# A decoder trunk on one core: x loaded ahead of the weights, and the first gate tile in two groups of k tiles

## The chip, the core and the metric

The kernel runs on one core of a Trainium2 chip. The metric is the device time of one execution in microseconds (us). A core has five engines that run their own queues of instructions: PE (TensorE, matrix products and transposes), DVE (VectorE), ACT (ScalarE), POOL (GpSimd) and SP (SyncE, which here issues nearly all DMAs). PEld in the profile is PE's loading of the operand that stays in the array.

## The reference: what is computed

Two layers of a trunk over 256 tokens with 1024 channels, in float32. Each layer is a half-step feed-forward block, a mixer of three groups of attention heads, and a second half-step feed-forward block. The change lies in the first feed-forward block of the first layer:

```
def rms_norm(x, g):
    y = xf * lax.rsqrt(jnp.mean(xf * xf, axis=-1, keepdims=True) + RMS_EPS)
    return (y * g.astype(jnp.float32)).astype(x.dtype)

def swiglu(x, w_gate, w_up, w_down):
    return (jax.nn.silu(x @ w_gate) * (x @ w_up)) @ w_down

h = h + 0.5 * swiglu(rms_norm(h, ffn1_norm[l]), ffn1_w_gate[l], ffn1_w_up[l], ffn1_w_down[l])
```

The gate and up matrices are 1024 x 2816, the down matrix 2816 x 1024.

## The kernel before

**Products in two parts.** A float32 operand is split in two fp32r tiles: a high part, which is a cast, and a low part, which is the float32 value minus the high part. A product is the sum of three: high by high, high by low, low by high. For weights, `W.high()` makes `wh` on ACT (line 117) and `W.low()` makes `wl` on DVE (line 121). For the activations, class `Norm` holds `xhl`, a tile of 8 k tiles by (high, low) by 256 tokens; `Norm.high` (line 318, ACT) multiplies the transposed x by the norm's gain and writes the high part, `Norm.low` (line 321, DVE) writes the low part. The division by the root of the mean square is applied later, behind the projection (`norm.sums`, `norm.broadcast`).

**A projection tile.** A tile of 128 hidden columns of gate or up takes, in `proj` (line 396), eight products of `wh` with high and low of x at once (512 columns, called wide here) into the two halves of one PSUM bank, and then eight products of `wl` with the high part (256 columns, called narrow) into the first half. `summed` (line 431) adds the halves.

**Loads.** All weights go through raw buffers that SP fills (line 91) in a fixed order, five in flight. x goes to `trunk` (token by channel) and is turned on PE with four 128 x 128 transposes per two k tiles (`Norm.turn`, line 324, transposes at line 329).

**The opening**, written out by hand. The constants with the identity matrix come on ACT's queue. SP issues: first quarter of x (256 of 1024 channels, 1 KB runs), lower half of the first gate tile (k tiles 0 to 3, 256 KB), second quarter of x, upper half of the gate tile, third and fourth quarters of x, the first up tile, the second gate tile, the second up tile. PE starts with 7 warm-up products of ones by ones, whose result nobody reads (line 1096), and then follows lines 1121 to 1138:

- `turn_x(0)`, the gains turned (`turn_gains`), 7 more warm-up products, `turn_x(1)`;
- for each quarter of x: its two products of `wh` by high (256 columns), two quarters ahead the next `turn_x`, then the products of `wl` by high, then of `wh` by low. The third and the fourth quarter are turned between the products of the first and the second.

ACT casts a half of the gate tile (line 1118) and then writes the high parts of a quarter; POOL subtracts to get `wl` of the gate tile (line 1119); DVE writes the low parts. Behind the gate tile (`g0`) `ffn` starts with the first up tile (`u0 = proj()`), then `g1`, `u1` and so on. ACT goes on with the casts of the next weights, then with the squares of x for the norm (line 344).

Of the kernel before, what the change touches and what calls it, by code (L numbers as in the profile page):

```python
# [18 lines left out]
P = 128  # L19
S = 256  # L20
D = 1024
KT = D // P
# [15 lines left out]
WARM = 7  # L38
# [103 lines left out]
def kernel(ctx: ExitStack, tc: tile.TileContext, x, ffn1_norm, ffn1_w_gate, ffn1_w_up, ffn1_w_down,  # L142
# [15 lines left out]
    V, A, G, T = nc.vector, nc.scalar, nc.gpsimd, nc.tensor  # L158

    def bank(tag):  # L160
        return psum.tile([P, 512], F32, name="ps_" + tag, tag=tag)
# [13 lines left out]
    def turn_gains(i):  # L175
        ps = bank("gu")
        T.transpose(ps[:, :16], rows[i], ident[:16, :16])
        V.tensor_copy(gT[:, 16 * i:16 * i + 16], ps[:, :16])

    ones = cp.tile([P, P], F32, name="ones")  # L180
# [2 lines left out]
    G.memset(minus_half, -0.5)  # L183
    nc.scalar.dma_start(cst[:, 0:P], const[:, 0:P])

    def load_x(mp):
        cols = slice(256 * mp, 256 * mp + 256)
        nc.sync.dma_start(trunk[:, :, cols], x[0].rearrange("(t p) d -> p t d", p=P)[:, :, cols])  # L188

    load_x(0)  # L190
    load_gains(0, ffn1_norm, nc.scalar)
    A.activation(tmp(P), ones, AF.Exp)
# [9 lines left out]
    W = Weights(tc, raw_pool, split_pool)  # L202
# [55 lines left out]
    W.by_hand = 2  # L258
    W.n_raw_done -= RAW_BUFS - 2
    W.issue()  # L260
    for mp in range(1, 4):
        if mp < 3:
            W.load(0, mp - 1)
        load_x(mp)
    W.load(1, 0)
    W.load(0, 2)
    W.load(1, 1)
# [25 lines left out]
    def mm(o, l, r, start, stop):  # L293
        T.matmul(o, l, r, start=start, stop=stop, skip_group_check=True)  # L294
# [789 lines left out]
    def before_mixer(l):  # L1084
        if l == 0:
            turn_gains(1)
            turn_gains(2)
            V.tensor_copy(identr, ident)
            V.memset(causal[:, P:2 * P], 0.0)
            for t in range(2):  # L1090
                V.tensor_scalar(causal[:, 2 * t * P:(2 * t + 1) * P], future, NEG, None, op0=ALU.mult)
        mixer_tables(l)

    warm = bank("gu")
    for i in range(WARM):
        mm(warm[:, :P], ones, ones, i == 0, i == WARM - 1)
    norm = Norm(0, 0)
    src, wh, wl = W.high_tiles()
    g0 = bank("gu").rearrange("p (a b) -> p a b", a=2)
    xT = []  # L1100

    def turn_x(mp):
        xT.append(norm.turn(mp))

    def gate(w, xs, ks):
        for k in ks:
            mm(g0[:, int(xs is norm.l)], w[:, k], xs[:, k], w is wh and xs is norm.h and k == 0,
               xs is norm.l and k == KT - 1)

    def first_norm(mp):  # L1110
        for i in range(2):
            norm.high(2 * mp + i, xT[mp][:, i])
        for i in range(2):
            norm.low(2 * mp + i, xT[mp][:, i])

    def split_gate(hf):
        ks = slice(4 * hf, 4 * hf + 4)
        A.copy(wh[:, ks], src[:, ks])
        G.tensor_tensor(wl[:, ks], src[:, ks], wh[:, ks].bitcast(F32), op=ALU.subtract)

    turn_x(0)
    turn_gains(0)
    for i in range(WARM):
        mm(warm[:, P:2 * P], ones, ones, False, i == WARM - 1)
    split_gate(0)
    first_norm(0)
    turn_x(1)
    split_gate(1)
    for mp in range(4):
        ks = range(2 * mp, 2 * mp + 2)  # L1130
        gate(wh, norm.h, ks)
        if mp < 2:
            turn_x(mp + 2)
        if mp > 0:
            gate(wl, norm.h, range(4) if mp == 1 else ks)
        gate(wh, norm.l, ks)
        if mp < 3:
            first_norm(mp + 1)
    W.low_done()
    W.take()  # L1140
    W.high()
# [8 lines left out]
    for l in range(DEPTH):  # L1150
        norm = ffn(norm, lambda: Norm(1, l), lambda: before_mixer(l), g0 if l == 0 else None)
        norm = mixer(l, norm, lambda: Norm(2, l))
        norm = ffn(norm, (lambda: Norm(0, l + 1)) if l + 1 < DEPTH else None)
# [35 lines left out]
```

## Time and profile before

| | |
|---|---|
| median of 3 runs | 1041.9 us (1041.54 to 1042.21) |
| the profiled execution's own time | 1041.75 us |
| its span, first to last instruction | 1039.8 us |
| HBM read | 179.67 MB, 174 GB/s over the span |
| ACT in the first 2.5% of the span | busy 6 tenths |
| DVE in the first 2.5% of the span | busy 4 tenths |

How to read the rows further down: in a timeline, the first number is the start in us from the start of the span, the second how long it took, then engine, line, operation, the tiles as out<-in, how many instructions the row merges, and in brackets how long the engine sat idle ahead of it and what ended that. A row that merges several instructions lasts from the first's start to the last's end. The ends of products are modelled and overlap the next one, so costs on PE are read from start to start. A row of DMA issues gives size and time from issue to landing. A row of a windows view gives the stretch, its length, the busy time and count of PE, PEld, DVE, ACT and POOL, the granted clock, the DMA engines' busy share and GB/s.

### The profile page before, as it was taken

The page shows a single profiled execution, that of the slowest core. Times are in us where ns is not written, and L with a number is a line of the kernel's source. Part 1 is how long each engine was busy: PE and PEld are TensorE (multiplying, and loading weights), DVE is VectorE, ACT ScalarE, POOL GpSimd, SP SyncE. Part 2 cuts the span into 40 slices and gives each one's busy share as a digit, 9 for nine tenths or more (in the row PEclk, how much of TensorE's full clock was granted, in tenths as well). Part 3 has the DMA queues.
Part 4 walks back from the last instruction along what each step waited for, and adds up shares of the span by engine and source line. Part 5 has one row for each costly group of instructions (what it writes and reads, how often), then busy time and mean ns, then how long its engine had stood idle before and what let it go on. Part 6 is the DMA issues. An engine that isn't in the chain of part 4 may idle for free.

```text
span 1039.8 us, 15145 instructions
## 1 busy us (share of the span) xinstructions
PE 1034.6 (100%) x5659; PEld 899.4 (86%) x5659; DVE 808.5 (78%) x1536; ACT 594.9 (57%) x1047; POOL 142.7 (14%) x173
## 2 busy tenths in 40 slices
PE   9999999999999999999999999999999999999998
PEld 8888888898888888888888888888988888888887
DVE  4997777789876887777788777777898768877775
ACT  6565555667754655555466555547667556555551
POOL 1003000167700000000000200002765000000000
PEclk9999999999999999999999999999999999999999
DMA  9675555555431374654646464555455214564631
GB/s 322 218 245 181 189 207 171 175 187 185 154 130 42 122 242 161 204 193 172 202 163 215 159 240 158 207 171 185 163 193 173 81 61 160 184 237 147 223 122 41
DMA packets 130905, 181.70 MB, mean 175 GB/s; under 512 B 7008, under 2 KB 104720, under 8 KB 130832
## 3 DMA queue, kind: packets, MB, share of 16 engines
q1 hardware_dynamic: 130656, 180.65, 51.0%
q8 instruction: 45, 0.74, 0.3%
q14 instruction: 28, 0.23, 0.1%
q10 hardware_dynamic: 176, 0.07, 0.0%
HBM read 179.67 MB, written 1.05 MB: 174 GB/s over the span
## 4 chain that ended last, share of the span: by engine, by line
PE 99%; DMA 1%; ACT 0%; SPq 0%; DVE 0%; issue 0%
PE ps_gu L294 66%; PE ps_acc L294 30%; PE ps_acc L329 1%; PE ps_gu L948 1%; PE ps_gu L1050 1%; DMA trunk<-in_x_dram 1%; PE ps_acc L649 0%; PE ps_acc L948 0%; PE ps_gu L981 0%; ACT wh L117 0%; SPq L91 0%; SPq L188 0%; PE ps_acc L355 0%; PE ps_acc L981 0%; DVE tmp L435 0%; DVE trunk L368 0%
## 5 line engine op out<-in xcount | busy, mean ns | idle before, releaser
L121 DVE TENSOR_TENSOR wl<-raw,wh 128x1024 fp32r<-128x1024 f32 (+2 forms) x343 | 416.6, 1220 | 29.2 <-ACT wh L117 29.0
L117 ACT CAST wh<-raw 128x1024 fp32r<-128x1024 f32 (+2 forms) x343 | 345.7, 1036 | 5.4 <-PE ps_gu L294 4.8
L294 PE MATMUL ps_gu<-xhl,wh 128*128 128x512 f32 (+1 forms) x1408 | 335.2, 389 | 0.2 <-DVE tmp L435 0.2
L294 PEld LDWEIGHTS ps_gu<-xhl,wh 128*128 128x128 f32 x1408 | 261.7, 188 | 53.2 <-DVE tmp L435 0.4
L294 PEld LDWEIGHTS ps_gu<-xhl,wl 128*128 128x128 f32 x1400 | 180.7, 191 | 7.2
L294 PE MATMUL ps_gu<-xhl,wl 128*128 128x256 f32 x1400 | 184.5, 283 | 0.0
L294 PE MATMUL ps_gu<-wh,xhl 128*128 128x512 f32 (+2 forms) x512 | 158.5, 379 | 0.0
L435 DVE TENSOR_TENSOR tmp<-ps_gu,tmp 128x256 f32<-128x256 f32 x175 | 72.5, 423 | 107.4 <-ACT tmp L434 107.2
L294 PE MATMUL ps_acc<-wh,hh 128*128 128x512 f32 (+1 forms) x352 | 137.7, 391 | 0.0
L294 PE MATMUL ps_acc<-wl,hh 128*128 128x512 f32 (+1 forms) x352 | 137.5, 391 | 0.0
L294 PE MATMUL ps_acc<-wh,hl 128*128 128x512 f32 (+1 forms) x352 | 136.5, 388 | 0.0
L434 ACT COPY tmp<-ps_gu 128x256 f32<-128x256 f32 x175 | 63.1, 371 | 93.9 <-PE ps_gu L294 93.8
L294 PEld LDWEIGHTS ps_gu<-wh,xhl 128*128 128x128 f32 x512 | 94.8, 188 | 14.5
L449 ACT CAST hh<-tmp 128x256 fp32r<-128x256 f32 x80 | 32.6, 407 | 119.9 <-DVE tmp L446 119.9
L294 PE MATMUL ps_gu<-wl,xhl 128*128 128x512 f32 (+2 forms) x256 | 95.7, 374 | 0.0
L305 POOL TENSOR_TENSOR y_n<-msq,minus_half 128x2 f32<-128x2 f32 x6 | 7.7, 1281 | 539.9 <-DVE msq L304 539.9
L441 ACT ACTIVATE tmp<-tmp 128x256 f32<-128x256 f32 x88 | 36.9, 419 | 77.8 <-DVE tmp L439 77.4
L294 PEld LDWEIGHTS ps_acc<-wh,hl 128*128 128x128 f32 x352 | 66.1, 188 | 14.0
L294 PEld LDWEIGHTS ps_acc<-wh,hh 128*128 128x128 f32 x352 | 66.4, 189 | 11.7
L294 PEld LDWEIGHTS ps_acc<-wl,hh 128*128 128x128 f32 x352 | 66.4, 189 | 11.4 <-DVE wl L121 0.7
L294 PEld LDWEIGHTS ps_gu<-wl,xhl 128*128 128x128 f32 x256 | 48.2, 188 | 6.6
L318 ACT ACTIVATE xhl<-ps_acc,gT 128x256 fp32r<-128x256 f32 x48 | 19.1, 475 | 37.2 <-PE ps_acc L329 37.1
(221 smaller groups left out, 1013.7 us busy)
## 6 DMA issues: line engine op xcount, KB each, us to landing
raw<-in_ffn_w_down_dram SPq DMA_DIRECT2D x44, 1024.0 KB, 4.9
raw<-in_ffn_w_gate_dram SPq DMA_DIRECT2D x43, 1024.0 KB, 6.7
raw<-in_ffn_w_up_dram SPq DMA_DIRECT2D x43, 1024.0 KB, 7.4
raw<-in_w_in_dram SPq DMA_DIRECT2D x24, 1024.0 KB, 5.0
raw<-in_w_out_dram SPq DMA_DIRECT2D x8, 1024.0 KB, 4.8
raw<-in_w_in_dram SPq DMA_DIRECT2D x4, 768.0 KB, 4.7
raw<-in_w_in_dram SPq DMA_DIRECT2D x4, 656.0 KB, 5.2
trunk<-in_x_dram SPq DMA_DIRECT2D x4, 256.0 KB, 4.7
```

The source lines that it names most:

```text
L117: self.nc.scalar.copy(hv, src)
L121: (engine or self.nc.vector).tensor_tensor(lv, self.srcs[self.n_low], hv.bitcast(F32), op=ALU.subtract)
L294: T.matmul(o, l, r, start=start, stop=stop, skip_group_check=True)
L305: G.tensor_tensor(y, dst, minus_half[:, :n], op=ALU.pow)
L318: A.activation(self.h[:, m], src, AF.Copy, scale=gT[:, self.col + m:self.col + m + 1])
L329: T.transpose(ps[:, i, t * P:(t + 1) * P], trunk[:, t, (2 * mp + i) * P:(2 * mp + i + 1) * P], ident)
L434: A.copy(o, ps[:, 1])
L435: V.tensor_tensor(o, ps[:, 0], o, op=ALU.add)
L441: A.activation(th, t_, AF.Tanh, scale=0.5)
L449: (V.tensor_copy if late else A.copy)(hh, t_)
L948: T.transpose(b[:, j * P:(j + 1) * P], pj[i][:, j * P:(j + 1) * P], ident)
L1050: T.transpose(b[:66, i * S + t * P:i * S + (t + 1) * P], src[t][:, 2 * hp_ + i, :], ident)
```

## The change

- x is loaded in two halves of 512 channels (2 KB runs), both issued ahead of every weight; then come both halves of the first gate tile, then the rest as before. SP issues two DMAs fewer.
- PE: 7 warm-up products as before; first quarter turned, gains turned, second quarter turned; 6 warm-up products; third and fourth quarter turned; 8 warm-up products. Only then the gate tile's products, in two groups of four k tiles: four wide products of `wh` with high and low, then four narrow ones of `wl` with high. That makes 8 products of 512 columns and 8 of 256 in place of 24 of 256, and 14 warm-up products in the place of 7 behind the first 7.
- ACT: the high parts of k tiles 0 to 3 come first, then the cast of the gate tile's lower half, then the high parts of k tiles 4 to 7.
- DVE: the low parts of k tiles 0 to 3, then the cast of the gate tile's upper half, which ACT did, then the low parts of k tiles 4 to 7.
- POOL: both subtractions as before.

```
-    def load_x(mp):
-        cols = slice(256 * mp, 256 * mp + 256)
+    def load_x(c):
+        cols = slice(512 * c, 512 * c + 512)
...
-    for mp in range(1, 4):
-        if mp < 3:
-            W.load(0, mp - 1)
-        load_x(mp)
+    load_x(1)
+    W.load(0, 0)
+    W.load(0, 1)
     W.load(1, 0)
...
+    def warm_up(n):
+        for i in range(n):
+            mm(warm[:, P:2 * P], ones, ones, False, i == n - 1)
...
-    def split_gate(hf):
+    def split_gate(hf, copy):
         ks = slice(4 * hf, 4 * hf + 4)
-        A.copy(wh[:, ks], src[:, ks])
+        copy(wh[:, ks], src[:, ks])
         G.tensor_tensor(wl[:, ks], src[:, ks], wh[:, ks].bitcast(F32), op=ALU.subtract)
...
-    turn_x(0)
-    turn_gains(0)
-    for i in range(WARM):
-        mm(warm[:, P:2 * P], ones, ones, False, i == WARM - 1)
-    split_gate(0)
-    first_norm(0)
-    turn_x(1)
-    split_gate(1)
-    for mp in range(4):
-        ks = range(2 * mp, 2 * mp + 2)
-        gate(wh, norm.h, ks)
-        if mp < 2:
-            turn_x(mp + 2)
-        if mp > 0:
-            gate(wl, norm.h, range(4) if mp == 1 else ks)
-        gate(wh, norm.l, ks)
-        if mp < 3:
-            first_norm(mp + 1)
+    for c in range(2):
+        xT.append(norm.turn(2 * c))
+        if c == 0:
+            turn_gains(0)
+        xT.append(norm.turn(2 * c + 1))
+        warm_up((6, 8)[c])
+        if c == 1:
+            split_gate(1, V.tensor_copy)
+        for mp in (2 * c, 2 * c + 1):
+            first_norm(mp)
+        if c == 0:
+            split_gate(0, A.copy)
+    for c in range(2):
+        for k in range(4 * c, 4 * c + 4):
+            mm(g0, wh[:, k], norm.x[:, k], k == 0, False)
+        for k in range(4 * c, 4 * c + 4):
+            mm(g0[:, 0], wl[:, k], norm.h[:, k], False, k == KT - 1)
```

More of the change, by code (lines that the diff above doesn't have):

```diff
@@ L1100 @@
     xT = []
[L1102 to L1108, printed above, removed]
+    def warm_up(n):
+        for i in range(n):
+            mm(warm[:, P:2 * P], ones, ones, False, i == n - 1)
     def first_norm(mp):
```

## The prediction

> **What bounds the kernel now.** I read the page's busy rows first, then its chain of work that ended last, then the list of waits of PE from 12 us to the end.
>
> ```profile
> span 1039.8 us, 15145 instructions
> ...
> PE 1034.6 (100%) x5659; PEld 899.4 (86%) x5659; DVE 808.5 (78%) x1536; ACT 594.9 (57%) x1047; POOL 142.7 (14%) x173
> ...
> PE 99%; DMA 1%; ACT 0%; SPq 0%; DVE 0%; issue 0%
> ```
> ```profile
> PE ps_gu L294 <- DVE tmp L435: 0.2, 1, 0.2
> ```
>
> PE is the bound from end to end. After 12 us it waits once, for 0.2 us; the one DMA in the chain (1%) is x in the opening. So nothing later waits for weights and could take in a shift: whatever PE gains or loses before its first full projection reaches the end almost unchanged. The whole question is **when PE starts the first up tile** (eight 512-wide products of u0 right behind the first gate tile). The timeline of the opening, first the issues and the first PE group, then PE alone:
>
> ```profile
> 0.72 0.44 SPq L188 DMA_DIRECT2D trunk<-in_x_dram  x1
> ...
> 0.98 3.29 PE L294 MATMUL ps_gu<-ones 128*128 128x128 f32 x14 [0.98 <-POOL minus_half L183]
> ...
> 1.22 0.48 SPq L91 DMA_DIRECT2D raw<-in_ffn_w_gate_dram  x1
> ...
> 1.74 0.50 SPq L188 DMA_DIRECT2D trunk<-in_x_dram  x1
> 2.28 0.47 SPq L91 DMA_DIRECT2D raw<-in_ffn_w_gate_dram  x1
> ```
> ```profile
> 4.19 0.63 PE L329 MATMUL ps_acc<-cst,trunk 128*128 128x128 f32 x4
> 4.75 0.23 PE L177 MATMUL ps_gu<-cst,tmp 16*128 16x16 f32 x1
> 4.91 1.83 PE L294 MATMUL ps_gu<-ones 128*128 128x128 f32 x14
> 6.57 0.60 PE L329 MATMUL ps_acc<-cst,trunk 128*128 128x128 f32 x4
> 6.93 0.48 PE L294 MATMUL ps_gu<-xhl,wh 128*128 128x256 f32 x2
> 8.21 0.66 PE L329 MATMUL ps_acc<-cst,trunk 128*128 128x128 f32 x4 [0.80 <-DMA trunk<-in_x_dram]
> 8.62 0.72 PE L294 MATMUL ps_gu<-xhl,wh 128*128 128x256 f32 x4
> ...
> 13.69 1.11 PE L294 MATMUL ps_gu<-xhl,wl 128*128 128x256 f32 x8
> 14.64 2.00 PE L294 MATMUL ps_gu<-xhl,wh 128*128 128x512 f32 x8
> 16.48 1.11 PE L294 MATMUL ps_gu<-xhl,wl 128*128 128x256 f32 x8
> ```
>
> Durations overlap, so costs are read from start to start. One warm-up call leaves two records (14 for 7 calls): 7 cost 6.57 - 4.91 = 1.66 us, 0.24 each. Four transposes cost 0.36 (6.57 to 6.93) to 0.41 (8.21 to 8.62). Eight wide products cost 16.48 - 14.64 = 1.84, 0.23 each; eight narrow ones 14.64 - 13.69 = 0.95, 0.12 each. u0's narrow products start at 13.69, so its wide ones started at 13.69 - 1.84 = **11.85**. In before PE stands idle about a microsecond in this stretch: the two products at 6.93 need 0.24, and the next group starts at 8.21, when the third quarter of x has landed.
>
> **The change part by part.**
>
> *When the first half of x lands.* The first three answers are the DMA issues at 0.72, 1.22 and 1.74, the fourth that at 2.28 (us to landing); then the DMA rate from 3 to 4 us, with 1 KB packets; then the rates in forty slices of 164 to 204 us, where 2 KB packets of w_in begin.
>
> ```profile
> trunk<-in_x_dram SPq DMA_DIRECT2D x1, 256.0 KB, 3.3
> raw<-in_ffn_w_gate_dram SPq DMA_DIRECT2D x1, 256.0 KB, 3.7
> trunk<-in_x_dram SPq DMA_DIRECT2D x1, 256.0 KB, 4.0
> raw<-in_ffn_w_gate_dram SPq DMA_DIRECT2D x1, 256.0 KB, 5.2
> 3.00:4.00 1.00, 1.00 (x7) 1.00 (x5) 0.00 (x0) 0.27 (x1) 0.00 (x0) 1.00 1.11 346
> GB/s 0 0 193 383 406 246 365 382 371 375 67 17 248 382 58 0 0 0 0 0 8 170 338 414 401 387 328 47 4 0 0 0 0 0 0 0 101 350 386 363
> ```
>
> They land at 0.72 + 3.3 = 4.02, 1.22 + 3.7 = 4.92, 1.74 + 4.0 = 5.74 and 2.28 + 5.2 = 7.48. A first transfer of twice the bytes ends 262 KB later: 0.65 us at the 406 GB/s of a good 2 KB slice, 0.76 at 346. Bounds: nothing (landing before the warm-ups end at 4.19, if the 3.3 us were all start-up), and 0.90, the step from 4.02 to 4.92. I take 0.65, nearest to the packets in question: landing 4.67, PE starts at **4.68 instead of 4.19**.
>
> *PE's work from there to u0.* The first warm-ups are unchanged. Then, in the order PE executes:
> - four transposes to the gains 0.56, gains 0.16, four transposes 0.40: 1.12;
> - 6 warm-ups 1.42, eight transposes 0.72, 8 warm-ups 1.90: 4.04;
> - two groups of four wide (0.92) and four narrow (0.48): 2.80.
>
> Together 7.96 us, u0 at 4.68 + 7.96 = **12.64**: 0.79 later than 11.85. Read against before: the start is 0.49 later; seven more warm-ups cost 1.66; about 1 us of idle time goes, and some hand-overs between sorts of matmul. The products themselves hardly change: before 24 of 256 columns at 0.12 = 2.88, after 2.80.
>
> *Whether anything else is later than PE.* Rows of the other engines:
>
> ```profile
> 4.91 0.62 ACT L1118 CAST wh<-raw 128x512 fp32r<-128x512 f32 x1 [1.64 <-DMA raw<-in_ffn_w_gate_dram]
> ...
> 5.43 0.83 ACT L318 ACTIVATE xhl<-ps_acc,gT 128x256 fp32r<-128x256 f32 x2
> 5.60 1.28 POOL L1119 TENSOR_TENSOR wl<-raw,wh 128x512 fp32r<-128x512 f32 x1 [4.30 <-ACT wh L1118]
> ...
> 8.90 2.67 DVE L321 SCALAR_TENSOR_TENSOR xhl<-ps_acc,gT,xhl 128x256 fp32r<-128x256 f32 x6 [1.73 <-PE ps_acc L329]
> ...
> 10.55 1.05 ACT L117 CAST wh<-raw 128x1024 fp32r<-128x1024 f32 x1
> ```
> ```profile
> L449 DVE CAST hh<-tmp 128x256 fp32r<-128x256 f32 x8 | 2.4, 295 | 0.3
> ```
>
> First group: ACT's first high part follows the gains by 5.43 - 4.75 = 0.68, so it starts at 4.68 + 0.56 + 0.68 = 5.92; four take 1.7 (0.83 for two), to 7.6. Only then comes ACT's cast of the gate tile's lower half, which has landed by then (second half of x 1.3 to 1.8 after the first, 6.0 to 6.5; then 256 KB in 0.76 to 0.90, 6.7 to 7.4): 8.2. POOL subtracts 1.28: 9.6. PE reaches the wide products at 4.68 + 5.16 = 9.84 and the narrow ones at 10.76, so both are covered, by over a microsecond. Without the warm-ups they would not be: the first product could not start before 8.2, which is 1.6 before 9.84.
>
> Second group: the new copy stands on DVE ahead of the last four low parts and waits for the upper half of the gate tile. That lands 0.76 after the lower one, or 1.74 as in before (7.48 - 5.74): 7.5 to 9.1. The copy of 512 columns is between the 0.30 of a 256-column cast and twice that; I take 0.45. Four low parts at 2.67 / 6 = 0.45 take 1.8, after the copy and after ACT's fifth and sixth high parts (8.2 + 0.83 = 9.05): done by 10.9 to 11.4. PE wants the first at 11.24 and the last at 11.93; covered by half a microsecond. POOL's second subtraction ends at 9.6 + 1.28 = 10.9, wanted at 12.16. The cover is gone when the upper half lands later than 12.64 - (0.45 + 1.8 + 0.23 + 0.48) = 9.7.
>
> u0's cast took 1.05 on ACT at 10.55; now ACT is free at 8.2 + 1.7 = 9.9, and the same bytes lie ahead of u0's tile on SP's queue, with two x issues fewer: ready by 11.6, wanted at 12.64. DVE's subtraction follows the low parts, wanted 1.84 later still. The squares read x later than any of this.
>
> So PE's own order is the bound, and the loss carries over: **+0.79 us**. The profiled execution took 1041.75 us (span 1039.8 and 1.95 around it), 0.15 under the median 1041.9 of the runs shown; the same shift on that median gives 1042.7.
>
> [...]
>
> ```profile
> 2.00:4.00 2.00, 2.00 (x11) 2.00 (x10) 0.00 (x0) 1.25 (x2) 0.00 (x0) 1.00 0.80 250
> ```
>
> The first 14 records took 4.19 - 0.98 = 3.21 us, 0.229 each, the same 14 later 0.119 each, though the granted clock reads 1.00 in both. PE idled about a microsecond before 8.21 and was as fast after. In the change PE idles from 4.19 to 4.68, just where it turned fast. [...]
>
> **The rivals.**
> - *Slower clearly: PE stays slow through the gap.* If the speed-up doesn't come at 4.19 because PE is idle then, another stretch like the first, 3.21 us, runs at 0.229 instead of 0.119 per record: 3.21 x (1 - 0.119 / 0.229) = 1.54 us more, +2.3, 1044.2. It decides if the speed-up needs PE busy past about 4.2. For it: the fast rows begin just there. Against: PE was busy for 3.2 us by then, as before.
> - *The gate tile's upper half is late.* If both halves needed 1.74, it would land at up to 6.5 + 3.5 = 10.0, past the 9.7 at which it decides: 0.3 more, up to 1 us if still later: 1043.0 to 1043.7. For it: the 7.48 of before. Against: two x transfers stand ahead of it no longer.
> - *No slower.* The landing costs nothing (u0 at 4.19 + 7.96 = 12.15, +0.30) and the stall below goes, because ACT and DVE now have 0.8 us more for the same work:
>
> ```profile
> 22.29 1.11 PE L294 MATMUL ps_acc<-xhl,wl 128*128 128x256 f32 x8
> 23.57 2.14 PE L294 MATMUL ps_gu<-xhl,wh 128*128 128x512 f32 x8 [0.17 <-DVE tmp L435]
> 25.55 1.10 PE L294 MATMUL ps_gu<-xhl,wl 128*128 128x256 f32 x8
> ```
>
>   Without it the group would start at 22.29 + 0.95 = 23.24 and take 1.84 instead of 1.98: 0.47. Both together: -0.17, 1041.7; one alone, 1042.2. Against: the work that ends the stall hangs on PE's own broadcast just ahead, and would move along.
>
> **How the numbers follow.** Forecast (+0.3 to +1.1 us, 1042.2 to 1043.0, predicted 1042.7): 0.68. Not slower: 0.12. Late gate tile: 0.08. Slow clock: 0.10. Something else: 0.02. The range 1041.7 to 1043.7 takes in the first three and leaves the slow clock out. 0.2% is 2.1 us, about what a measurement of this kernel can tell from no change: faster than 1039.8 has 0.01, slower than 1044.0 has 0.11 (the slow clock and a remainder), within 0.88.
>
> **What would show it.** Right: transposes of x start at 4.6 to 4.9; PE then runs without idling, warm-ups included, to u0's first wide product at 12.3 to 12.9; the low parts end before PE wants them; the stall before the first 512-wide group behind the broadcast is still there. Wrong: idle time of PE ahead of a wide product (then a copy, low part or landing is late, and its releaser says which); warm-up records of 0.2 us after 4.7 (slow clock); u0 before 11.85 (then my landing or the cost of the warm-ups is too high).

## The result and the profile after

| | before | after |
|---|---|---|
| median | 1041.88 us (7 runs, 1041.54 to 1042.21) | 1045.22 us (7 runs, 1042.80 to 1045.45) |
| profiled execution, span | 1041.75, 1039.8 | 1044.92, 1043.1 |

The ratio after to before is 1.0028, 95% interval 1.0018 to 1.0038: slower by 3.3 us. The prediction said 1042.7 with a range to 1043.7, and gave 1044.2 to one rival, a PE that stays slow through its gap. Six of the seven runs lie between 1044.92 and 1045.45, one at 1042.80, which is the forecast's place. The page of the changed kernel, busy rows and chain:

```profile
span 1043.1 us, 15156 instructions
PE 1037.9 (99%) x5665; PEld 902.1 (86%) x5665; DVE 809.9 (78%) x1537; ACT 593.9 (57%) x1046; POOL 143.1 (14%) x173
...
PE 99%; DMA 0%; ACT 0%; DVE 0%; issue 0%
```

PE is the bound as before. Its waits from 12 us on, then its timeline in the opening:

```profile
PE ps_gu L293 <- DVE tmp L434: 0.2, 1, 0.2
```
```profile
0.98 3.36 PE L293 MATMUL ps_gu<-ones 128*128 128x128 f32 x14 [0.98 <-POOL minus_half L183]
5.08 1.08 PE L328 MATMUL ps_acc<-cst,trunk 128*128 128x128 f32 x4 [0.75 <-DMA trunk<-in_x_dram]
6.10 0.28 PE L177 MATMUL ps_gu<-cst,tmp 16*128 16x16 f32 x1
6.31 1.11 PE L328 MATMUL ps_acc<-cst,trunk 128*128 128x128 f32 x4
7.22 2.46 PE L293 MATMUL ps_gu<-ones 128*128 128x128 f32 x12
9.52 1.04 PE L328 MATMUL ps_acc<-cst,trunk 128*128 128x128 f32 x8
10.39 1.95 PE L293 MATMUL ps_gu<-ones 128*128 128x128 f32 x16
12.10 1.17 PE L293 MATMUL ps_gu<-xhl,wh 128*128 128x512 f32 x4
...
14.96 2.00 PE L293 MATMUL ps_gu<-xhl,wh 128*128 128x512 f32 x8
```

u0 starts at 14.96, 3.11 later than the 11.85 of before; the profiled executions differ by 1044.92 - 1041.75 = 3.17. So the loss is made before 15 us and carried to the end, as predicted. From 5.08 to u0 PE does not wait once. It works slowly: the first four transposes with the gains' one take 6.31 - 5.08 = 1.23 us, where the forecast had 0.72, and the 12 warm-up records take 9.52 - 7.22 = 2.30, 0.19 each, where it had 0.12. Then the same work is fast: eight transposes in 0.87, 16 warm-up records in 1.71.

How x landed. The first row is the issue at 0.72 alone, the second gives the median of both issues, 0.72 and 1.19, so the second half took about 5.0:

```profile
trunk<-in_x_dram SPq DMA_DIRECT2D x1, 512.0 KB, 4.2
trunk<-in_x_dram SPq DMA_DIRECT2D x2, 512.0 KB, 4.6
```

The first half is there at 0.72 + 4.2 = 4.92 and PE starts 0.16 later; forecast were 4.67 and 4.68.

### The profile page after: what moved, and what is told of

It reads as the page before. It is cut to its first block, busy times and chain, and to the rows that moved or that the text cites. A ratio compares the mean times of both kernels' runs of the same rounds, so it can differ in the third digit from the quotient of the medians.

```text
span 1043.1 us, 15156 instructions
## 1 busy us (share of the span) xinstructions
PE 1037.9 (99%) x5665; PEld 902.1 (86%) x5665; DVE 809.9 (78%) x1537; ACT 593.9 (57%) x1046; POOL 143.1 (14%) x173
## 4 chain that ended last, share of the span: by engine, by line
PE 99%; DMA 0%; ACT 0%; DVE 0%; issue 0%
PE ps_gu L293 66%; PE ps_acc L293 30%; PE ps_acc L328 1%; PE ps_gu L947 1%; PE ps_gu L1049 1%; DMA trunk<-in_x_dram 0%; PE ps_acc L648 0%; PE ps_acc L947 0%; PE ps_gu L980 0%; ACT wh L117 0%; PE ps_acc L354 0%; PE ps_acc L980 0%; PE ps_gu L177 0%; DVE tmp L434 0%; DVE trunk L367 0%; ACT rb L356 0%
## 5 line engine op out<-in xcount | busy, mean ns | idle before, releaser
L293 PE MATMUL ps_gu<-xhl,wh 128*128 128x512 f32 x1400 | 334.7, 390 | 0.2 <-DVE tmp L434 0.2
L293 PEld LDWEIGHTS ps_acc<-wl,hh 128*128 128x128 f32 x352 | 66.4, 189 | 11.4 <-DVE wl L121 0.7
```

## The experiments

**Theory A**: PE's records turn from about 0.21 us to 0.11 us (12 of them in 2.56 and in 1.34 us, rows below) at a moment that differs from run to run and depends, as I supposed, on PE having been busy for a while; the changed kernel, whose PE idles 0.75 us ahead of 5.08, usually misses the early moment, and its long row of PE work ahead of u0 has no wait in it that could hide slow records. **Rival B**: the moment is fixed by PE's work. **Rival C**: the gap does nothing, and what costs is the new order itself, the warm-ups, or the late x. Medians are in us. Runs of before beside them had medians of 1041.87 (first four experiments), 1041.72 (the next four) and 1041.45 (the last four).

### The kernel before, profiled again

> The kernel before, unchanged, for a second look at when its PE records turn from 0.21 us to 0.11 us each (4.1 us in the first profile). [...] Rival B (the moment is fixed by the work, PE having been busy for 3.1 us): 4.1 us again.

1041.78. PE in this execution:

```profile
4.13 0.96 PE L329 MATMUL ps_acc<-cst,trunk 128*128 128x128 f32 x4
5.02 0.23 PE L177 MATMUL ps_gu<-cst,tmp 16*128 16x16 f32 x1
5.18 1.83 PE L294 MATMUL ps_gu<-ones 128*128 128x128 f32 x14
6.85 0.60 PE L329 MATMUL ps_acc<-cst,trunk 128*128 128x128 f32 x4
...
8.31 0.66 PE L329 MATMUL ps_acc<-cst,trunk 128*128 128x128 f32 x4 [0.63 <-DMA trunk<-in_x_dram]
...
13.80 1.11 PE L294 MATMUL ps_gu<-xhl,wl 128*128 128x256 f32 x8
```

Here the first transposes were still slow (0.89 to the gains, 0.56 in the first profile), and the second four started 0.28 later. But PE then waits for the third quarter of x, which landed 0.1 later this time, and u0 starts at 13.80 - 1.84 = 11.96, 0.11 later than in the first profile. So the moment isn't fixed in the kernel before either, against B, and in this execution **the wait for x hides it**. That idle time, which the prediction booked as a gain of the change, was the cover of a slow PE.

Not every execution of before is so even. Of the 86 timed beside all the experiments and the result, ten lie apart, at 1043.37 to 1043.78, and none between 1042.48 and 1043.37. None of the ten was profiled, so whether the turn came too late there for the wait to hide it is open.

### The changed kernel again

> The changed kernel, unchanged, again. Theory A: most runs near 1045.2 with fast records from about 9 us, a minority near 1042.8 with fast records before 5.1 us, and none between 1043.3 and 1044.3, because the only PE activity that can turn it fast lies either ahead of the gap or well behind it. [...]

1044.61; ratio 1.0028 (1.0017 to 1.0038). The seven runs: 1043.03, 1043.04, 1043.32, 1044.61, 1045.29, 1045.33, 1045.40. Two groups with nothing between 1043.32 and 1044.61, close to what theory A had. The profiled execution is of the first group (1043.04), which shows the other case:

```profile
5.01 0.63 PE L328 MATMUL ps_acc<-cst,trunk 128*128 128x128 f32 x4 [0.68 <-DMA trunk<-in_x_dram]
5.57 0.23 PE L177 MATMUL ps_gu<-cst,tmp 16*128 16x16 f32 x1
...
6.22 1.50 PE L293 MATMUL ps_gu<-ones 128*128 128x128 f32 x12
7.56 1.04 PE L328 MATMUL ps_acc<-cst,trunk 128*128 128x128 f32 x8
...
10.14 1.17 PE L293 MATMUL ps_gu<-xhl,wh 128*128 128x512 f32 x4
...
12.99 2.00 PE L293 MATMUL ps_gu<-xhl,wh 128*128 128x512 f32 x8
```

The same program, the same order, PE fast from its first transpose: first transposes to u0 takes 12.99 - 5.01 = **7.98**, against 14.96 - 5.08 = **9.88** in the first profile. The difference lies in two pieces: up to the warm-ups 1.21 against 2.14, and the 12 warm-up records 1.34 against 2.30, together 1.89. This is one program with two times, 1.88 us apart, and PE's pace ahead of u0 accounts for the difference.

### The gap filled

```
-WARM = 7
+WARM = 11
```

> The changed kernel with 11 instead of 7 warm-up products ahead of x, so that PE does not idle from 4.1 to 5.1 us. [...] Rival B (the gap has nothing to do with it; more warm-ups only delay the transposes): transposes start about 0.8 us later, fast records still at about 9 us, time 1045.5 to 1046.

1043.62 (ten runs, 1043.16 to 1044.22); ratio 1.0017 (1.0008 to 1.0027). PE from the first warm-up to the first transposes, and u0:

```profile
0.98 4.47 PE L293 MATMUL ps_gu<-ones 128*128 128x128 f32 x22 [0.98 <-POOL minus_half L183]
5.29 0.60 PE L328 MATMUL ps_acc<-cst,trunk 128*128 128x128 f32 x4
...
13.26 2.00 PE L293 MATMUL ps_gu<-xhl,wh 128*128 128x512 f32 x8
```

The transposes start 0.2 later than with the gap, and the time is 1.6 us less. No run comes near 1045.2. More warm-ups ahead of x, more work for PE in all, and a faster kernel: against C, the gap is a cause. This run changes the gap and the number of warm-ups at once; the run with x in quarters, below, closes the gap with the 7 warm-ups kept.

### The gap made longer

```
-WARM = 7
+WARM = 3
```

> The changed kernel with 3 instead of 7 warm-up products ahead of x: PE idles from 2.3 to 5.0 us. Theory A: no run turns fast ahead of the transposes, fast records only at 8 to 10 us; all runs between 1044.9 and 1046, none near 1042.8. If the gap plays no part: the same mixture as the changed kernel, some runs near 1042.8.

1045.33 (four runs: 1044.60, 1045.33, 1045.34, 1045.51); ratio 1.0036 (1.0022 to 1.0050). No run of the first group, though four runs are few (4 of 14 of the changed kernel were of it), and one was 0.3 under what was expected. The warm-up records behind the gap take 9.65 - 7.09 = 2.56 for 12, and the turn comes only within the eight transposes that start at 9.65 (1.19 in place of 0.87), later than with 7:

```profile
4.95 1.08 PE L328 MATMUL ps_acc<-cst,trunk 128*128 128x128 f32 x4 [2.32 <-DMA trunk<-in_x_dram]
...
7.09 2.77 PE L293 MATMUL ps_gu<-ones 128*128 128x128 f32 x12
9.65 1.36 PE L328 MATMUL ps_acc<-cst,trunk 128*128 128x128 f32 x8
10.84 1.95 PE L293 MATMUL ps_gu<-ones 128*128 128x128 f32 x16
```

### The later warm-ups taken out

```
-        warm_up((6, 8)[c])
```

> The changed kernel without the 6 and the 8 warm-up products behind the first 7. If the later warm-ups stand in the way (theory C: PE has nothing better to do only up to 9.2 us, the rest is their own cost, doubled while PE is slow): first up tile at 12.7 to 13.3, limited by the low parts on DVE, time 1042.8 to 1043.4. If they are what makes PE fast (theory A in its strict form: without them PE is busy too little and stays slow well past 9 us): products at 0.43 and 0.21 us each, first up tile at 14 or later, time 1044.5 or more.

1042.83 (ten runs, 1042.17 to 1043.02); ratio 1.0006 (0.9997 to 1.0015). 2.4 us under the changed kernel, with the gap still there: the 14 later warm-up products, which I supposed would keep PE fast, cost more than they gave; PE was as fast here without them (four wide products of the gate tile in 1.20 us, 1.17 in the changed kernel). Without them PE waits for ACT, for POOL and then for the low parts:

```profile
8.17 1.20 PE L293 MATMUL ps_gu<-xhl,wh 128*128 128x512 f32 x4 [0.80 <-ACT wh L1113]
9.54 0.74 PE L293 MATMUL ps_gu<-xhl,wl 128*128 128x256 f32 x4 [0.17 <-POOL wl L1114]
10.22 1.74 PE L293 MATMUL ps_gu<-xhl,wh 128*128 128x512 f32 x4
```

So slow records would have something to hide behind, as in before. PE was fast from 5.00 in this profiled execution (1042.23, u0 at 12.27), so the hiding itself isn't shown by it; what speaks for it is that all ten runs lie within 0.85 us, where the two groups of the changed kernel are about 2 us apart. Of rival C this part holds: the later warm-ups do cost, beside the gap.

### x in quarters, all ahead of the weights

```
-        cols = slice(512 * c, 512 * c + 512)
+        cols = slice(256 * c, 256 * c + 256)
...
-    load_x(1)
+    for c in range(1, 4):
+        load_x(c)
```

> The changed kernel with x in four quarters of 1 KB runs, all four still ahead of the weights. The first transposes then need 256 KB and start at 4.1 to 4.3, so PE has no gap. Theory A: fast records between 3.8 and 7.2, first up tile at 12.1 to 13.6, time 1042.2 to 1043.8. Rival (the gap is not the cause, the order of PE's work is): 0.9 us earlier than the changed kernel because of the landing alone, 1044.3.

1042.71; ratio 1.0008 (0.9998 to 1.0018). Nine of ten runs lie between 1042.10 and 1043.20, as theory A has it; one at 1045.19 is not explained. The transposes start at 4.13, so PE has no gap, with 7 warm-ups as in the changed kernel; they are slow (1.20 to the second four), and the 12 warm-up records are fast:

```profile
4.13 1.06 PE L329 MATMUL ps_acc<-cst,trunk 128*128 128x128 f32 x4
...
5.33 1.00 PE L329 MATMUL ps_acc<-cst,trunk 128*128 128x128 f32 x4
...
6.17 1.50 PE L294 MATMUL ps_gu<-ones 128*128 128x128 f32 x12
```

Here x is also there earlier, so what speaks for the gap is that the slow group is all but gone, and not the whole gain.

### The same without the later warm-ups

```
-        cols = slice(512 * c, 512 * c + 512)
+        cols = slice(256 * c, 256 * c + 256)
...
-    load_x(1)
+    for c in range(1, 4):
+        load_x(c)
...
-        warm_up((6, 8)[c])
```

> The changed kernel with x in four quarters ahead of the weights and without the later 14 warm-up products. PE starts at 4.1 and has slack behind each transpose, so a late turn to fast records is hidden. Gate tile lands at about 8.1 and 8.8 as in the run with quarters; DVE's cast of the upper half waits for POOL and ends at about 10.4; low parts by 12.0, first up tile at 12.5 to 12.8: 1042.4 to 1042.8. Rival (only warm-ups keep PE fast): 1043.5 or more.

1042.14 (1041.84 to 1042.61); ratio 1.0005 (0.9995 to 1.0014): 0.4 over the runs of before beside it, so 2.9 of the 3.3 us are gone, and it is no better than before. It came out under what was expected.

### The load order alone

The kernel before, with every engine's instructions in the old order:

```
-        cols = slice(256 * mp, 256 * mp + 256)
+        cols = slice(512 * mp, 512 * mp + 512)
...
-    for mp in range(1, 4):
-        if mp < 3:
-            W.load(0, mp - 1)
-        load_x(mp)
+    load_x(1)
+    W.load(0, 0)
+    W.load(0, 1)
```

> The kernel before with the new load order alone (x in two halves ahead of the gate tile), the instructions of every engine in the old order. ACT's first cast then waits for the gate tile's lower half at about 7.0 with all high parts queued behind it, so they end at about 11.6 and the low parts at 12.0: first up tile at 12.4 or later, and up to 14 where PE, idle from 4.1 to 5.0, stays slow. Theory A: 1042.4 to 1044. Rival (the load order costs only the later landing of x, 0.9 us): 1042.7 in every run, none later.

1042.96 (1042.22 to 1044.21); ratio 1.0014 (1.0005 to 1.0023). ACT, with high parts queued behind its first cast:

```profile
7.11 0.62 ACT L1117 CAST wh<-raw 128x512 fp32r<-128x512 f32 x1 [3.79 <-DMA raw<-in_ffn_w_gate_dram]
7.63 0.83 ACT L317 ACTIVATE xhl<-ps_acc,gT 128x256 fp32r<-128x256 f32 x2
```

Runs spread over 2 us again, with PE's gap; not one value for every run, as the rival had it.

### The order of work alone

The changed kernel with the loads of before:

```
-        cols = slice(512 * c, 512 * c + 512)
+        cols = slice(256 * c, 256 * c + 256)
...
-    load_x(1)
-    W.load(0, 0)
-    W.load(0, 1)
+    for mp in range(1, 4):
+        if mp < 3:
+            W.load(0, mp - 1)
+        load_x(mp)
```

> The changed order of work on all engines with the old loads (quarters of x between the halves of the gate tile). PE has no gap ahead of x. The third and fourth quarters of x land at 8.2 and 8.8, and 8 warm-ups and all products stand behind them: 8.2 + 1.0 for turning + 1.9 + 2.8 = first up tile at 13.9, whatever PE's speed before 8 us: 1043.7 to 1044.0, with a spread under 0.7. Rival (only the loads did harm): 1042.3 or less.

1043.46 (1043.24 to 1044.18); ratio 1.0014 (1.0005 to 1.0024). The third quarter of x was turned at 8.12 and the fourth right behind it; turning and warm-ups took 2.58 where I had reckoned 2.9, and u0 starts at 13.56. The time came out under what was expected, with a spread of 0.94. So each half of the change costs by itself, the load order 1.24 over the runs of before beside it and the order of work 1.74. That the sum, 2.98, is near the 3.3 shows no more than that: the second cost has no gap in it (PE idles 0.23 ahead of its first transposes).

### Attempts at something better than before

One DMA of before moved: the gate tile's upper half behind all of x, cast behind the third quarter's high parts.

```
+    W.load(0, 0)
     for mp in range(1, 4):
-        if mp < 3:
-            W.load(0, mp - 1)
         load_x(mp)
+    W.load(0, 1)
...
     turn_x(1)
-    split_gate(1)
...
             first_norm(mp + 1)
+        if mp == 1:
+            split_gate(1)
```

> The kernel before with one DMA moved: the gate tile's upper half is issued after all of x, and ACT casts it behind the high parts of the third quarter. If before is bound by the third and fourth quarters of x (landed at 8.2 and 8.8): they land 0.7 to 0.9 earlier, first up tile at 11.3 to 11.6, time 1041.3 to 1041.6. If it is bound by the gate tile's upper half (landing at 8.8 now, POOL's 1.28 behind it): first up tile at 11.8 or later, 1041.9 to 1042.3.

1042.41; ratio 1.0006 (0.9997 to 1.0016): a miss, near the second case. x came earlier (third quarter turned at 7.67), but PE waits for POOL's second subtraction, which the later cast pushed back:

```profile
11.31 0.50 PE L294 MATMUL ps_gu<-xhl,wl 128*128 128x256 f32 x2 [0.85 <-POOL wl L1119]
```

In before that subtraction ends at 9.49 (8.20 + 1.29) and PE first reads its result at 10.58; the cast, moved from 7.51 to 9.29, used up this cover of 1.1 us and more. Moving one path ahead only made the other late.

Then x in two halves, 9 warm-ups ahead and none later, both casts on ACT between the high parts of the halves (against the changed kernel).

```
-WARM = 7
+WARM = 9
...
-        warm_up((6, 8)[c])
-        if c == 1:
-            split_gate(1, V.tensor_copy)
...
             split_gate(0, A.copy)
+            split_gate(1, A.copy)
```

> x in two halves first, 9 warm-up products ahead of it and none later, and both casts of the gate tile on ACT, between the high parts of the two halves. If what is left of the loss is the casts' and low parts' path: ACT casts end at 8.6, high parts at 10.2, low parts at 10.7, POOL's second subtraction at 10.8; first up tile at 11.4 to 11.6, time 1041.3 to 1041.6. If PE's own speed still decides (late fast records without later warm-ups): first up tile at 12.2 or later, 1042.2 or more.

1042.47 (1041.99 to 1042.69); ratio 1.0008 (0.9999 to 1.0017). Another miss. In the profiled execution PE was slow until about 7 us (the second four transposes started at 6.33 and not at 5.7), which is 0.6 of the delay; u0 started at 12.60, 1.0 to 1.2 later than hoped. The rest is likely the low parts, which ended at 11.67 (10.01 + 1.66) where 10.7 was expected. None of the eleven runs came under 1041.99, so PE's pace alone is not what was missed. No version beat before.

### POOL and the new copy

The changed kernel without the later warm-ups, and `wl` of the lower half made by DVE.

```
-        warm_up((6, 8)[c])
...
-    def split_gate(hf, copy):
+    def split_gate(hf, copy, engine):
...
-        G.tensor_tensor(wl[:, ks], src[:, ks], wh[:, ks].bitcast(F32), op=ALU.subtract)
+        engine.tensor_tensor(wl[:, ks], src[:, ks], wh[:, ks].bitcast(F32), op=ALU.subtract)
...
-            split_gate(1, V.tensor_copy)
+            split_gate(1, V.tensor_copy, G)
...
-            split_gate(0, A.copy)
+            split_gate(0, A.copy, V)
```

> The changed kernel without the 14 later warm-ups, and with the lower half's subtraction on DVE instead of POOL, so that POOL is idle while DVE casts the upper half. If DVE's 1.3 us for that cast is a wait for POOL's subtraction beside it: 0.3 to 0.5 now, low parts done by 11.1, first up tile at 11.7 to 12.0, 1041.6 to 1042.0. If the cast itself takes 1.3: low parts by 12.0, first up tile at 12.7, 1042.6 or more.

1042.70 (1041.97 to 1042.85); ratio 1.0010 (1.0000 to 1.0019). The cast of the upper half took 0.42. Next to it, DVE and POOL of the changed kernel:

```profile
9.26 0.68 DVE L1114 TENSOR_TENSOR wl<-raw,wh 128x512 fp32r<-128x512 f32 x1
9.86 0.42 DVE L1113 CAST wh<-raw 128x512 fp32r<-128x512 f32 x1
```
```profile
9.13 1.31 DVE L1113 CAST wh<-raw 128x512 fp32r<-128x512 f32 x1
```
```profile
8.89 1.27 POOL L1114 TENSOR_TENSOR wl<-raw,wh 128x512 fp32r<-128x512 f32 x1 [7.58 <-ACT wh L1113]
```

So 0.89 of the cast's 1.31 us came of POOL's subtraction beside it: POOL starts here at 10.37, behind the cast's end at 10.28. The time did not follow: in this profiled execution (1042.85) PE was slow until its last transposes had ended, about 9 us, and u0 started at 12.78. Two of the ten runs, 1041.97 and 1041.99, came to the 1042.0 that was expected; that PE's pace is what held up the others is likely but not shown.

## Why the prediction was wrong, point by point

- **What bounds the kernel: right.** The time is u0's start and a constant. Time minus u0's start is 1029.90 in before (1041.75 - 11.85), 1029.82 in its second profile, 1029.96 in the changed kernel, 1030.05 in its second profile, 1030.08 with the gap filled. Nothing later takes in a shift, and the 0.2 us stall behind the broadcast stayed (row of waits above).
- **When x lands: the size was off.** PE's start was forecast at 4.68 and measured at 5.08 and 5.01: 0.4 of the loss. Of this 0.25 is the landing (4.92 for 4.67) and 0.16 the step from landing to first transpose, for which the sum had 0.01. The rate was not what failed: the DMA engines moved 399 GB/s between 4 and 5 us, and 406 was charged. But from 2 us to 4.92 they moved about 0.84 MB (142, 329 and 399 GB/s in the three stretches, an estimate), while the half itself is 0.52 and the constants and gains, on ACT's queue, 0.07: the rest belongs to what SP issued behind the half, and the sum counted the half's own bytes alone. The bound of 0.90, from the step between the first two landings, was the better row: 4.02 + 0.90 = 4.92.
- **PE's work up to u0, 7.96 in the sum: this is the step that failed.** It took 9.88 in the first profile and 7.98 in the second, whose records are fast throughout:

  | | forecast | first profile | second profile |
  |---|---|---|---|
  | eight transposes and the gains | 1.12 | 2.14 | 1.21 |
  | 6 warm-ups | 1.42 | 2.30 | 1.34 |
  | the next eight transposes | 0.72 | 0.87 | 0.87 |
  | 8 warm-ups | 1.90 | 1.71 | 1.71 |
  | the gate tile's products | 2.80 | 2.86 | 2.85 |

  Not the count was wrong but the price: each transpose and warm-up was taken at the fast price, from rows of before in which PE had been working without a gap, and the first two terms came out 1.9 and 1.6 times as long. The sum for the usual run is 0.79 + 0.40 for x + 1.92 here = 3.11, which is what u0 lost. That 7.98 lies so near to 7.96 is partly luck, since single terms miss by up to 0.19 and cancel.
- **Whether anything else is later than PE: right as to the outcome.** PE waited for nothing from 5.08 on. The copy on DVE was priced at 0.45 and takes 0.42 alone, but 1.31 beside POOL; the low parts ended at 12.69 where 11.4 was the latest expected. PE, late itself, began the second group at 13.57 and never met that; in the second profile they ended at 11.32 and PE took them from 11.60 on, so it was no wait there either. Without the later warm-ups the low parts were the next in line: the second four wide products take 11.79 - 10.22 = 1.57 there in place of 0.91.
- **The slow rival.** What this rival named, PE slow behind its gap, is what happened in the first profile and, by their times, in 10 of the 14 runs of the changed kernel (those from 1044.61 up). Its price, 1.54, was nearer than its chance, 0.10: it let PE stay slow for 3.21 us more, and PE stayed slow from 5.08 to about 9.2. That a second slow stretch would be as long as the first was an assumption that no run shows. The prediction calls this rival the slow clock; the granted clock reads 1.00 in the slow stretch and behind it (7 to 8 us and 10 to 11 us of the changed kernel), and what is slow is the spacing of PE's records. What was held against it, that PE had been busy for 3.2 us "as before", is where the judgement went wrong: the kernel before doesn't need to be fast at 4.2, and its second profile shows an execution that wasn't. One profile showed the turn just at the gap and I took the place as given.
- **The other rivals.** The late gate tile did not occur (DVE's cast of its upper half started at 9.13, just as late as the low parts ahead of it allowed). The no-slower case did not occur.

The turn is not at one place in one kernel: PE is fast from 4.2 and from about 5 in two profiles of before, by 5.0 or only from about 9.2 in two of the changed kernel. What sets its place was not shown. That PE's having been busy brings it about is my supposition; what the runs show is the medians, 1043.62 with 11 warm-ups ahead of x, 1045.22 and 1044.61 with 7, 1045.33 with 3. No run shows the bounds of 3.8 and 7.2 us that an expectation (x in quarters) gives the turn; the profiles have it from 4.2 to about 10.3.

A late turn does not need a gap: it came at about 6.2 with x in quarters and at about 7 with 9 warm-ups and hardly a gap. Of the profiles that have a gap and missed the early turn, the turns are at about 9, 9.2 and 10.3; no profile without one shows it so late. And idle time behind the turn did no such harm: with quarters and no later warm-ups PE idled 1.17 us ahead of its first wide products, and four of them took 1.19, as in the fast rows.

## What to carry to other kernels

An idle stretch of the bounding engine can be the cover of a cost that varies from run to run; before it is booked as a gain, ask what it hides, and profile a second execution. Warm-up work did better here ahead of the first data that PE has to wait for (1043.62 us with 11 products there, 1045.22 and 1044.61 with 7); placed behind it, where nothing else is later than PE, it delayed all that follows (1045.22 and 1044.61 with the 14 later products, 1042.83 without), and nearly twice as much while PE is still slow (2.56 against 1.34 us for 6 products here). Where two loads feed the same products, as x and the weights do here, find out how much cover the one has before the other is put ahead of it.

## What the runs showed of the hardware that was not expected

- The granted clock reads 1.00 in the slow stretch too (row below); the slow PE is seen in the spacing of its records (2.56 / 12 = 0.21 us for one of 128 columns with the gap made longer, 1.34 / 12 = 0.11 in the second profile of the changed kernel). The row of 7 to 8 us of the changed kernel, granted clock third from the end:

```profile
7.00:8.00 1.00, 1.00 (x6) 1.00 (x6) 0.50 (x2) 1.00 (x4) 0.00 (x0) 1.00 1.15 347
```

- The DVE cast of 128x512 that started while POOL subtracted took 1.31 us in place of 0.42 and ended at 10.44, 0.28 after POOL's 10.16. In four more profiles it took 1.26 to 1.52 and ended 0.28 or 0.29 after POOL (9.72 and 10.00 with the gap filled, 9.48 and 9.77 without the later warm-ups, 10.12 and 10.41 with x in quarters, 9.66 and 9.94 with quarters and no later warm-ups). The prediction did not reckon with it.
